# A hybrid decoder step on one core: weight splits on an absolute pace, waiting stores issued a step later, a third buffer for decay rows, sample states loaded ahead

## The chip, the cores and the metric

The kernel runs on one core of a Trainium2 chip. The metric is the time of one execution on the device in microseconds (us). The page below counts five engines: PE is TensorE's matmuls, PEld its weight loads, DVE is VectorE, ACT is ScalarE, POOL is GpSimd. SP is SyncE, which here does nothing but issue DMA transfers, one after the other; POOL issues some as well.

## The reference, cut to what matters

One layer: a half-step gated FFN, a token mixer of two gated branches (windowed pooling, and a state-space scan with a causal convolution), and a second half-step FFN, all in float32. There are 1024 prompt tokens and 8 sequences of 8 new tokens ("samples") that start from a stored state.

```
def swiglu(x, w_in, w_out):                     # D_MODEL 1024, D_FF 2816
    gu = x @ w_in
    g, u = gu[..., :D_FF], gu[..., D_FF:]
    return (jax.nn.silu(g) * u) @ w_out
def ssd_scan(x, dt, A, bm, cm, h0):             # 32 heads of 64, 4 groups, state 128, chunks of 128 tokens
    ...
    y_diag = jnp.einsum('bcgrls,bcsgrp->bclgrp', cb[:, :, :, None] * decay, xdt)
    st = jnp.einsum('bclgn,bclgr,bclgrp->bcgrpn', br, decay_end, xdt)
    h_last, h_prev = lax.scan(step, h0, ...)    # h * chunk_decay + st, chunk after chunk
    y_off = jnp.einsum('bclgn,bcgrpn,bclgr->bclgrp', cr, h_prev, jnp.exp(a_cs))
    return y_diag + y_off, h_last
def layer(x, pool_hist, out_pos0, conv_hist, h0, l):
    x = x + 0.5 * swiglu(rmsnorm(x, norm_ffn1[l]), ffn1_w_in[l], ffn1_w_out[l])
    mix, new_pool, new_conv, new_ssm = token_mixing(rmsnorm(x, norm_mix[l]), ...)
    x = x + mix
    x = x + 0.5 * swiglu(rmsnorm(x, norm_ffn2[l]), ffn2_w_in[l], ffn2_w_out[l])
    return x, new_pool, new_conv, new_ssm       # then a last rmsnorm
```

## The kernel before, in words

Tokens are cut into two halves, h = 0 (512 prompt tokens) and h = 1 (512 and the 64 sample tokens). Every weight and every operand is split into two parts, a rounded one (`wh`, `hi`, made by ACT) and the rest (`wl`, `lo`, made by DVE from the first), and a product is three matmuls: hi*wh, lo*wh, hi*wl. The wide projections use a seven-product scheme on 2x2 blocks (`wino`, tiles `pw`), whose block sums POOL makes (`s`, L443).

The stages, in order of time: **FFN 1 in** (products `pg`, `pu`, then `pw`; hidden rows go to DRAM as `hd`), **FFN 1 out** (`po`: first h = 0, then h = 1; hidden rows come back as `hr` through POOL's queue and are split into `hh` and `hr`), the **mixer's projections** (`pz`, `pw`: pool rows u, gate rows z, convolution rows, gates), the **mix stage** (the scan in 8 prompt chunks and one sample chunk for each of 4 groups, beside the pooling products `pgm` and `pbp`, the scan's output product `pso` and the merged output `pwo`), and **FFN 2**, built as FFN 1.

While FFN 1 runs, `part_weights` (L303) splits 90 weight pieces of the mixer and of FFN 2's start ahead of time: a load of 256 KB (`wr`), an ACT copy (`wp`, L352), a DVE subtraction (`wr`, L354), and two stores of 256 KB into DRAM (`wp<-wp`, `wp<-wr`, L314 and L315). Later stages load these pieces ready-made (`wraw<-wp`, `wh<-wp`, `wl<-wp`, L290).

The order on the engines comes from three things. The code is written as generators ("chains"). `pe[0]` is a clock that the program keeps while it is written out: each matmul adds its columns divided by 2400, so it runs in planned us, a little faster than the chip. A chain yields a delay, and `tick()`, called after each few matmuls, runs the chains that are due; a chain that is `finish`ed is written out at once, without matmuls between. Last, a scheduler places each engine's instructions by readiness and priority. Once placed, each engine, and SP's queue of transfers too, works strictly in its order: an instruction that waits holds everything behind it.

In the mix stage, `ssd_load` (L1277) loads the decay rows `ab` of a chunk, 512 KB, into one of two buffers. `ssd_a` (L1286) makes exponentials from them on ACT (`ea` L1299, eight Relu rows L1301, one Exp L1302), transposes x and B on PE (`pxT`, `pcb`) and copies B's transposition (`btok`, L1325). `ssd_m` multiplies `ab` by the masked products (L1337). `ssd_st` is the state product (`pst`); `ssd_b` makes the chunk's output (`pyo`, `pyd`). For the sample chunk `ssd_b` goes through eight units: load 256 KB of stored state (`h<-in_state_ssm_dram`, L1356), transpose (`ph0T`), products (`pyos`, `pnew`), add, store (`out_dram<-h`, L1389). `fin` (L1448, L1449) is the group's last prompt state. `gating` norms the result with `rstd` (a matmul `pss`, three Newton steps on DVE, a transposition `prt`, and a trip through DRAM, `rd` and `r`) and stores it as `yd`. In `u_pair`, POOL packs the last rows for the new pool state (`cst`, L984) and PE transposes them (`pust`).

Of the kernel before, what the change touches and what calls it, by code (L numbers as in the profile page):

```python
# [14 lines left out]
P = 128  # L15
# [46 lines left out]
G_WAIT = (4.0, 5.0)  # L62
H_AT, H_PACE, H_LAND = 2.0, (0.4, 0.68), 3.5
W_AT, W_LAND, W_NEXT = 105.0, 2.4, 1.7
# [3 lines left out]
def tile_hybrid_pool_ssd_macaron(  # L68
# [211 lines left out]
    def load_w(w, k0, nk, c0, ncol=P, raw=None, pin=False):  # L280
# [15 lines left out]
        with tc.high_priority(hp[0]):  # L296
            d = S.activation(wh, raw, AF.Copy)  # L297
            if pin:
                tc.keep_in_program_order(d)
            V.tensor_tensor(wl, raw, wh.bitcast(F32), op=ALU.subtract)  # L300
# [79 lines left out]
    def rstd(tiles, h, count, out, pace=1.0, sums=None, waits=None):  # L380
# [31 lines left out]
        S.copy(rt[:nch], pt[:nch, :P])  # L412
        dma(rd[:nch], rt[:nch])
# [189 lines left out]
    def ffn(wi, wo, prep, after, half=None, sums=None):  # L603
# [9 lines left out]
        def inner(h):  # L613


            N = NTOK[h]
            parts = [], []
            todo = []

            def cut():  # L620
                _, t, a = todo.pop(0)
                split(t, a[:, :N], t.bitcast(F32R))

            for k in range(NFF):
                own = k < 3 if h == 0 else not half and k >= NFF - 2
                t, a = (fx(d, n_) if own else act((P, 576), d, n_) for d, n_ in ((F32, "hr"), (F32R, "hh")))
                t = t[:, :N]
                G.dma_start(t, hdram[h][k])
                parts[0].append(a)
                parts[1].append(t.bitcast(F32R))  # L630
                todo.append((pe[0], t, a))
                yield H_PACE[h]
                while todo and todo[0][0] + H_LAND < pe[0]:
                    cut()
            while todo:
                yield max(0.3, todo[0][0] + H_LAND - pe[0])
                cut()
            return parts
# [7 lines left out]
        for h in HALVES:  # L646
# [3 lines left out]
            for ms in ((0, 1),) + tuple((m,) for m in range(2, KD)):  # L650
# [39 lines left out]
    def load_x(h, out):  # L690
# [31 lines left out]
        for i, (_, c0, c) in enumerate(blocks):  # L722
            V.tensor_scalar_mul(dg[i][:c, :c], ident[:c, :c], ss[:c, 2, i : i + 1])
        if h == 1:
# [86 lines left out]
    for _ in range(4):  # L811
# [152 lines left out]
    def u_pair(k0, sin, ost):  # L964
# [4 lines left out]
        def mean(h, k, raw):  # L969
# [5 lines left out]
            else:  # L975
# [8 lines left out]
                G.tensor_copy(st[:, HIST:].rearrange("p (b t) -> p b t", t=NT), raws[:, :, HIST:])  # L984
                pt = psum("ps", "pust")
# [199 lines left out]
    def load_dts(h):  # L1185

        t, cd = act((P, 480), name="dts"), small((P, 128), "cd", 2)
# [14 lines left out]
    def mix_pool(h):  # L1202
# [11 lines left out]

        def out(m):
            t0 = act((P, N), name="t0")
# [4 lines left out]
            dma(accd[h][m], t0)  # L1221
# [3 lines left out]
        for m in range(KD):  # L1225
# [8 lines left out]
            out(m)  # L1234

# [41 lines left out]

    def ssd_load(h, g, c):
# [453 lines left out]
```

## Time and profile before

| | us |
|---|---|
| median of 3 runs (lowest to highest) | 3009.23 (3006.12 to 3012.07) |
| the profiled execution | 3018.36 |
| its span, first to last instruction | 3016.4 |
| PE busy / DVE / ACT / POOL | 2877.0 / 1608.8 / 1314.1 / 858.0 |
| mean granted TensorE clock | 0.980 |

The page's second part shows the stages: each digit is the busy share of a fortieth of the span (75.4 us) in tenths.

```profile
PE   7999999898999999999999889998999999998998
...
PEclk9999999999999999999999989999999999999999
DMA  4487667896363333333368888788775222235442
```

Counted from 0, slices 7 to 9 are FFN 1 out and its two seams, slices 21 to 27 the mix stage, and slice 36 is the seam inside FFN 2. DMA is the busy share of the 16 engines that move the data.

### The profile page before, as it was taken

How to read it: one execution, taken by the hardware profiler on the slowest of the kernel's cores; microseconds unless marked ns; L12 is line 12 of the kernel's file. 1: busy time of each engine (PE TensorE's matmuls, PEld its weight loads, DVE VectorE, ACT ScalarE, POOL GpSimd, SP SyncE). 2: the span in 40 equal slices, each digit the busy share in tenths (PEclk: the TensorE clock that was granted, in tenths of full speed). 3: DMA queues.
4: the chain of work that ended last, by engine and by line, in shares of the span. 5: the costliest groups of instructions: out<-in, count | busy, mean ns of one | idle time of the engine just before them, and what ended most of it. 6: DMA issues, size and time to landing. Idle time of an engine off the chain costs nothing.

```text
span 3016.4 us, 54111 instructions
## 1 busy us (share of the span) xinstructions
PE 2877.0 (95%) x20356; PEld 2710.4 (90%) x20356; DVE 1608.8 (53%) x2834; ACT 1314.1 (44%) x2755; POOL 858.0 (28%) x917
## 2 busy tenths in 40 slices
PE   7999999898999999999999889998999999998998
PEld 6999999678989999999987787778999999997898
DVE  6554445545255576666647755663256343444532
ACT  5344444433233355555556745541123333343422
POOL 5333334000053333333313232342115333341000
PEclk9999999999999999999999989999999999999999
DMA  4487667896363333333368888788775222235442
GB/s 134 140 264 230 203 206 228 279 287 221 100 199 115 104 98 116 97 101 105 109 196 289 271 258 268 255 251 277 261 258 159 86 82 69 83 107 183 156 141 72
DMA packets 531225, 532.34 MB, mean 176 GB/s; under 512 B 41531, under 2 KB 371377, under 8 KB 530955
## 3 DMA queue, kind: packets, MB, share of 16 engines
q1 hardware_dynamic: 523906, 504.37, 52.5%
q0 software_dynamic: 7040, 24.52, 2.3%
q8 instruction: 160, 2.62, 0.4%
q14 instruction: 103, 0.84, 0.1%
q10 hardware_dynamic: 16, 0.00, 0.0%
HBM read 377.09 MB, written 151.90 MB: 175 GB/s over the span
## 4 chain that ended last, share of the span: by engine, by line
PE 75%; DMA 7%; issue 6%; DVE 4%; ACT 2%; POOL 2%; SPq 1%; ACTq 0%; DVEq 0%; POOLq 0%
PE pw L166 45%; PE po L166 10%; PE pso L166 6%; PE pwo L166 3%; PE pu L166 2%; PE pg L166 2%; DMA wr<-in_ffn_w_in_dram 1%; PE pbp L166 1%; PE pz L166 1%; DMA hr<-hd 1%; PE pyos L166 1%; DMA wraw<-wp 1%; PE pyd L166 1%; ACT ab L1301 1%; DMA wr<-in_w_o_dram 1%
## 5 line engine op out<-in xcount | busy, mean ns | idle before, releaser
L166 PE MATMUL pw<-hi,wh 128*128 128x288 f32 (+1 forms) x2176 | 630.6, 290 | 9.9 <-DVE t L554 9.5
L166 PE MATMUL pw<-hi,wl 128*128 128x288 f32 (+1 forms) x2176 | 628.9, 289 | 0.4 <-DVE wl L450 0.4
L166 PE MATMUL pw<-lo,wh 128*128 128x288 f32 (+1 forms) x2176 | 628.4, 289 | 0.0
L166 PE MATMUL pw<-X,wh 128*128 128x256 f32 (+1 forms) x3264 | 626.1, 290 | 2.1 <-ACT rb L842 1.3
L166 PEld LDWEIGHTS pw<-X,wh 128*128 128x128 f32 x3264 | 517.9, 191 | 3.2 <-ACT rb L842 1.7
L166 PE MATMUL pw<-X,wl 128*128 128x256 f32 (+1 forms) x1632 | 472.2, 289 | 0.1
L166 PEld LDWEIGHTS pw<-hi,wh 128*128 128x128 f32 x2176 | 412.8, 190 | 10.8 <-DVE t L554 10.2
L166 PEld LDWEIGHTS pw<-hi,wl 128*128 128x128 f32 x2176 | 412.8, 190 | 0.6 <-DVE wl L450 0.6
L166 PEld LDWEIGHTS pw<-lo,wh 128*128 128x128 f32 x2176 | 412.9, 190 | 0.0
L450 DVE TENSOR_TENSOR wl<-s,wh 128x512 fp32r<-128x512 f32 x284 | 204.9, 722 | 262.5 <-ACT wh L449 258.4
L166 PEld LDWEIGHTS pw<-X,wl 128*128 128x128 f32 x1632 | 311.8, 191 | 0.3 <-DVE wl L450 0.3
L443 POOL TENSOR_TENSOR s<-wraw,wraw 128x512 f32<-128x512 f32 x142 | 196.0, 1380 | 404.3 <-DVE wl L450 278.5
L166 PE MATMUL po<-hh,wh 128*128 128x288 f32 (+1 forms) x1056 | 292.4, 331 | 13.1 <-ACT wh L297 13.1
L449 ACT ACTIVATE wh<-s 128x512 fp32r<-128x512 f32 x284 | 179.7, 633 | 274.8 <-PE pw L166 220.5
L166 PE MATMUL po<-hh,wl 128*128 128x288 f32 (+1 forms) x1056 | 291.3, 331 | 5.2 <-DVE wl L300 4.6
L166 PE MATMUL po<-hr,wh 128*128 128x288 f32 (+1 forms) x1056 | 289.7, 329 | 0.0
L300 DVE TENSOR_TENSOR wl<-wraw,wh 128x512 fp32r<-128x512 f32 x216 | 142.5, 665 | 227.3 <-ACT wh L297 225.5
L297 ACT ACTIVATE wh<-wraw 128x512 fp32r<-128x512 f32 x216 | 127.1, 598 | 271.7 <-PE po L166 241.9
L450 DVE TENSOR_TENSOR wl<-wraw,wh 128x512 fp32r<-128x512 f32 x213 | 161.0, 756 | 104.0 <-ACT wh L449 96.3
L449 ACT ACTIVATE wh<-wraw 128x512 fp32r<-128x512 f32 x213 | 134.6, 632 | 179.9 <-PE pw L166 163.0
L166 PEld LDWEIGHTS po<-hh,wh 128*128 128x128 f32 x1056 | 181.0, 190 | 30.6 <-ACT wh L297 17.5
L166 PEld LDWEIGHTS po<-hh,wl 128*128 128x128 f32 x1056 | 180.4, 189 | 26.9 <-DVE wl L300 13.3
(390 smaller groups left out, 5204.9 us busy)
## 6 DMA issues: line engine op xcount, KB each, us to landing
wraw<-in_ffn_w_in_dram SPq DMA_DIRECT2D x184, 256.0 KB
wraw<-wp SPq DMA_DIRECT2D x180, 256.0 KB
wraw<-in_ffn_w_out_dram SPq DMA_DIRECT2D x160, 256.0 KB
wraw<-in_w_in_dram SPq DMA_DIRECT2D x124, 256.0 KB
wp<-wp SPq DMA_DIRECT2D x90, 256.0 KB
wp<-wr SPq DMA_DIRECT2D x90, 256.0 KB
wh<-wp SPq DMA_DIRECT2D x90, 256.0 KB
wl<-wp SPq DMA_DIRECT2D x90, 256.0 KB
```

The costliest lines, as they stand in the source:

```text
L166: T.matmul(out, lhsT, rhs, start=start, stop=stop, skip_group_check=free)
L297: d = S.activation(wh, raw, AF.Copy)
L300: V.tensor_tensor(wl, raw, wh.bitcast(F32), op=ALU.subtract)
L443: G.tensor_tensor(t, a, b, op=op)
L449: S.activation(wh, a, AF.Copy)
L450: V.tensor_tensor(wl, a, wh.bitcast(F32), op=ALU.subtract)
L1301: S.activation(ab[:L, i, :], ab[:L, i, :], AF.Relu, bias=acs[:L, hc + i : hc + i + 1], scale=-1.0)
```

## The change

It removes and adds no transfer: SP issues 1977 rows before and after, and the matmuls are the same. It moves work, in seven groups:

- **Start.** DVE subtracts the first three pinned weight pieces (`wl`) after the row norms of h = 0 instead of before them.
- **Early splits.** `part_weights` works on a pace of 4.3 planned us a piece from a fixed start; before, it waited 2.4 and then 1.7 after each step, and every wait rounded up to the next `tick`. Load, split and store of a piece are one step apart each, and a piece's store is written ahead of the next piece's split.
- **FFN out.** The hidden rows are split at a set pace, and the products of `po` start with the rows that are split, where before all 22 were split first.
- **Stores a step later.** `rd`, `accd`, `out_dram<-h`, `fin`, `yd` and `xspill` are written one step after the work that makes them.
- **Transpositions later.** `pust` four planned us after the packing; `pss` and `prt` of the gating by (5.0, 8.0) where it was (4.0, 5.0).
- **Decay rows.** A third `ab` buffer, and the load a chunk earlier. `cbm`, `btok` and `cd` move from a pool of their own into the 58 shared `act` slots. `btok` is copied ahead of the Relu rows.
- **Sample states.** The first three of a group are loaded when its sample chunk begins, and the two empty steps that stood between load and use are gone.

```diff
-G_WAIT = (4.0, 5.0)
-H_AT, H_PACE, H_LAND = 2.0, (0.4, 0.68), 3.5
-W_AT, W_LAND, W_NEXT = 105.0, 2.4, 1.7
+G_WAIT = (5.0, 8.0)
+H_AT, H_PACE, H_LAND, H_CUT = 2.0, (0.4, 0.68), 5.0, 0.9
+W_AT, W_NEXT = 108.0, 4.3
...
-        for w, k0, nk, c0, ncol in jobs:
-            t, a = fx(name="wr")[:, : nk * ncol], fx(F32R, name="wp")[:, : nk * ncol]
-            dma(t.rearrange("p (k c) -> p k c", c=ncol),
-                w[k0 * P : (k0 + nk) * P, c0 : c0 + ncol].rearrange("(k p) c -> p k c", p=P))
-            yield W_LAND
-            split(t, a, t.bitcast(F32R))
-            yield W_NEXT
-            d = dp.tile([P, 2, 4 * P], F32, tag=f"wp{len(parted)}", name=nm("wp"))
-            dma(d[:, 0, : nk * ncol], a.bitcast(F32))
-            dma(d[:, 1, : nk * ncol], t)
-            parted[id(w), k0, c0] = d
+        held, t0 = {}, pe[0]
+        for i in range(len(jobs) + 2):
+            if i < len(jobs):
+                w, k0, nk, c0, ncol = jobs[i]
+                t = fx(name="wr")[:, : nk * ncol]
+                dma(t.rearrange("p (k c) -> p k c", c=ncol),
+                    w[k0 * P : (k0 + nk) * P, c0 : c0 + ncol].rearrange("(k p) c -> p k c", p=P))
+                held[i] = t, fx(F32R, name="wp")[:, : nk * ncol]
+            if i >= 2:
+                ...
+                dma(d[:, 0, : nk * ncol], a.bitcast(F32))
+                dma(d[:, 1, : nk * ncol], t)
+                parted[id(w), k0, c0] = d
+            if 1 <= i <= len(jobs):
+                t, a = held[i - 1]
+                split(t, a, t.bitcast(F32R))
+            yield max(0.1, t0 + W_NEXT * (i + 1) - pe[0])
...
         S.copy(rt[:nch], pt[:nch, :P])
+        yield 1.0
         dma(rd[:nch], rt[:nch])
...
+            while k < NFF or todo:
+                if k < NFF:
+                    ...
+                    G.dma_start(t, hdram[h][k])
+                    todo.append((pe[0], t, a))
+                    k += 1
+                    yield H_PACE[h]
+                while todo and todo[0][0] + H_LAND < pe[0] and last + H_CUT < pe[0] or k == NFF and todo:
+                    if k == NFF:
+                        yield max(0.2, todo[0][0] + H_LAND - pe[0], last + H_CUT - pe[0])
+                    _, t, a = todo.pop(0)
+                    split(t, a[:, :N], t.bitcast(F32R))
+                    parts[0].append(a)
+                    parts[1].append(t.bitcast(F32R))
+                    last = pe[0]
...
-                    finish(hid[h])
-                    parts = hid[h].value
+                    hid[h].step() if not hid[h, "parts"] else None
+                    parts = hid[h, "parts"]
...
                         for kk in range(n4):
+                            while len(parts[0]) <= kb + kk:
+                                hid[h].step()
                             products([pts], wh, wl, kk, slice(0, P), [(h, *parts)], kb + kk, NFF)
...
+        if h == 0:
+            yield 0.0
...
-    for _ in range(4):
+    for _ in range(6):
         prep1[0][0].step()
...
                 G.tensor_copy(st[:, HIST:].rearrange("p (b t) -> p b t", t=NT), raws[:, :, HIST:])
+                yield 4.0
                 pt = psum("ps", "pust")
...
         def out(m):
+            if done:
+                later(1.5, lambda d=done.pop(): dma(*d))
             t0 = act((P, N), name="t0")
             ...
-            dma(accd[h][m], t0)
+            done.append((accd[h][m], t0))
...
-        ab = stage["p"].tile([P, HPG, P], F32, tag="ab", bufs=2, name=nm("ab"))[:, :, :L]
+        ab = stage["p"].tile([P, HPG, P], F32, tag="ab", bufs=3, name=nm("ab"))[:, :, :L]
...
-        cbm = small((P, P), "cbm", 2)
+        cbm = act((P, P), name="cbm")
...
-            h0s = {i: load(units[i]) for i in range(N_H0)}
-            yield STEP_S
-            yield STEP_S
             hTs = {0: turn(h0s[0], units[0])}
...
+                if last:
+                    dma(*last.pop())
                 dst = new_ssm_s[0, bh * 4 : bh * 4 + 4, 2 * gp : 2 * gp + 2].rearrange("b h p n -> (h p) b n")
-                dma(dst, h0)
+                last.append((dst, h0))
+            yield STEP_S
+            dma(*last.pop())
...
         for c in range(n):
-            a = yield from ssd_a(h, g, c, ab, Bf, Cf, xs4, dts)
+            cur = ab
+            if c + 1 < n:
+                ab = ssd_load(h, g, c + 1)
+            if c == 4:
+                for i in range(N_H0):
+                    h0s[i] = state_load(g, i)
+            a = yield from ssd_a(h, g, c, cur, Bf, Cf, xs4, dts)
             yield step
             if prev:
-                yield from ssd_b(h, g, *prev, Cf, y4, dts)
-            if c + 1 < n:
-                ab = ssd_load(h, g, c + 1)
+                yield from ssd_b(h, g, *prev, Cf, y4, dts, h0s)
...
             S.copy(fo, pt)
+            yield step
             dma(new_ssm_p[0, 0, g * HPG : (g + 1) * HPG].rearrange("(q h) p n -> (h p) q n", h=2),
...
-            dma(yd[h][k], y)
             yield GP[1]
+            if j:
+                dma(yd[h][k - 1], y4[:, j - 1, :N])
...
-            dma(xspill[h][m], x_)
+            if m:
+                dma(xspill[h][m - 1], out[m - 1])
```

Three places of the engines' order, before and now. In the rows a name left of the arrow is written, one right of it read; the numbers tell tiles apart.

ACT at the seam of FFN 1 in and FFN 1 out for h = 0, from the first hidden row (`hh<-hr`) on. `wp<-wr` is an early split, `wh<-wraw` a weight of `po`. Before:

```order
L352 ACTIVATE hh_6707<-hr_6706 128x512
L352 ACTIVATE wp_6734<-wr_6733 128x512
L352 ACTIVATE hh_6737<-hr_6736 128x512
L297 ACTIVATE wh_6931<-wraw_6929 128x512
L352 ACTIVATE hh_6758<-hr_6757 128x512
L352 ACTIVATE hh_6782<-hr_6781 128x512
L352 ACTIVATE hh_6809<-hr_6808 128x512
L557 ACTIVATE g_6683<-g_6683 128x288
L352 ACTIVATE hh_6839<-hr_6838 128x512
```

Now:

```order
L361 ACTIVATE hh_6830<-hr_6829 128x512
L361 ACTIVATE hh_6854<-hr_6853 128x512
L297 ACTIVATE wh_6968<-wraw_6966 128x512
L361 ACTIVATE wp_6879<-wr_6877 128x512
L361 ACTIVATE hh_6875<-hr_6874 128x512
L297 ACTIVATE wh_7038<-wraw_7036 128x512
L361 ACTIVATE hh_6905<-hr_6904 128x512
L567 ACTIVATE g_6800<-g_6800 128x288
L297 ACTIVATE wh_7068<-wraw_7066 128x512
```

The weights of `po` moved up among the hidden rows. Of the 90 early splits 62 stand ahead of the first row shown and 28 behind it before the change; now it is 78 and 12, the last of them behind 16 of h = 0's 48 weight pieces.

SP at the first sample chunk (group 0 of h = 1). Before, the three state loads stand behind eight loads of scan outputs (`y<-yd`):

```order
L1489 DMA y_21198<-yd_0_193 128x512
L1489 DMA y_21201<-yd_1_194 128x512
L1489 DMA y_21204<-yd_2_195 128x512
L1221 DMA accd_5_110<-t_3518_21101 128x576
L1489 DMA y_21207<-yd_3_196 128x512
L1489 DMA y_21210<-yd_4_197 128x512
L1489 DMA y_21213<-yd_5_198 128x512
L1489 DMA y_21216<-yd_6_199 128x512
L1489 DMA y_21219<-yd_7_200 128x512
L1356 DMA h_3551_21251<-in_state_ssm_dram 128x4x128
L1356 DMA h_3552_21253<-in_state_ssm_dram 128x4x128
L1356 DMA h_3553_21255<-in_state_ssm_dram 128x4x128
```

Now:

```order
L1549 DMA z_20983<-zd_148 128x576
L1302 DMA h_3497_20989<-in_state_ssm_dram 128x4x128
L1302 DMA h_3498_20991<-in_state_ssm_dram 128x4x128
L1302 DMA h_3499_20993<-in_state_ssm_dram 128x4x128
L290 DMA wl_21107<-wp_3541 128x512
L1499 DMA yd_12_205<-y_3310_20075 128x512
L1232 DMA accd_4_109<-t_3483_20935 128x576
```

They moved 24 rows up, ahead of all the loads of `y`.

SP after the last group's prompt state, in the output product of h = 0. Before, the store of `fin` stands ahead of the second half of the weight piece that PE is using (`wraw_23970`) and of all that follow:

```order
L1389 DMA out_dram<-h_4106_23814 128x4x128
L1389 DMA out_dram<-h_4110_23835 128x4x128
L1449 DMA out_dram<-fin_23956 128x4x128
L290 DMA wraw_23970<-wp_7390 128x512
L290 DMA wh_23991<-wp_7431 128x512
L290 DMA wl_23993<-wp_7431 128x512
```

Now:

```order
L1405 DMA out_dram<-h_4104_23802 128x4x128
L1409 DMA out_dram<-h_4110_23827 128x4x128
L1475 DMA out_dram<-fin_23954 128x4x128
L1619 DMA xspill_4_85<-x_4059_23587 128x512
L290 DMA wh_23988<-wp_6730 128x512
L290 DMA wl_23990<-wp_6730 128x512
```

The store still stands ahead of weight loads, but the first of them, `wh_23988`, is now the piece that PE reaches 15 matmuls after the transposition of `fin`; before, it was one that PE needed in the very next matmul.

On PE, `pust` stood one row behind the transposition `puh` of the same channel block (four of eight blocks) or 14 to 19 behind it; now it stands 25 to 37 rows behind.

More of the change, by code (lines that the diff above doesn't have):

```diff
@@ L616, in inner @@
             N = NTOK[h]
[L617 to L638, printed above, removed]
+            parts = hid[h, "parts"] = [], []
+            todo, last = [], 0.0
+            k = 0
+            while k < NFF or todo:
+                if k < NFF:
+                    own = k < 3 if h == 0 else not half and k >= NFF - 2
+                    t, a = (fx(d, n_) if own else act((P, 576), d, n_) for d, n_ in ((F32, "hr"), (F32R, "hh")))
+                    t = t[:, :N]
+                    G.dma_start(t, hdram[h][k])
[10 more added lines that the diff above has]
+                    last = pe[0]
         hid = {}
@@ L1185, in load_dts @@
     def load_dts(h):
-        t, cd = act((P, 480), name="dts"), small((P, 128), "cd", 2)
+        t, cd = act((P, 480), name="dts"), act((P, 128), name="cd")
         dma(t, dts_d[h][:, :480])
@@ L1234, in mix_pool @@
             out(m)
+        dma(*done.pop())
     def load_group(h, g):
@@ L1276, in sample_parts, with state_load @@
             yield STEP_S
+    SAMPLE_UNITS = [(pr, bh) for pr in range(4) for bh in range(2)]
+    def state_load(g, i):
+        pr, bh = SAMPLE_UNITS[i]
+        gp = g * 4 + pr
+        t = act((P, 4, P), name="h0")
+        dma(t, state_ssm[0, bh * 4 : bh * 4 + 4, 2 * gp : 2 * gp + 2].rearrange("b h p n -> (h p) b n"))
+        return t
     def ssd_load(h, g, c):
         L = NS if c == 4 else CH
-        ab = stage["p"].tile([P, HPG, P], F32, tag="ab", bufs=2, name=nm("ab"))[:, :, :L]
+        ab = stage["p"].tile([P, HPG, P], F32, tag="ab", bufs=3, name=nm("ab"))[:, :, :L]
         src = acs_sd[g * HPG : (g + 1) * HPG] if c == 4 else acs_d[h][c, g * HPG : (g + 1) * HPG]
@@ L1295, in ssd_a @@
         hcs = slice(hc, hc + HPG)
-        ea = act((P, 4, L), name="ea")
-        av = ab.rearrange("p (q h) l -> p q h l", h=2)
-        for hh in range(2):
-            S.activation(ea[hh * HD : (hh + 1) * HD], av[hh * HD : (hh + 1) * HD, :, hh, :], AF.Exp)
-        for i in range(HPG):
-            S.activation(ab[:L, i, :], ab[:L, i, :], AF.Relu, bias=acs[:L, hc + i : hc + i + 1], scale=-1.0)
-        S.activation(ab[:L], ab[:L], AF.Exp, scale=-1.0)
         px = psum("ps", "pxT")
@@ L1309, in ssd_a @@
             tr(pb[:L, 128:256], Bf[:, tok], ident)
+        ea = act((P, 4, L), name="ea")
+        av = ab.rearrange("p (q h) l -> p q h l", h=2)
+        for hh in range(2):
+            S.activation(ea[hh * HD : (hh + 1) * HD], av[hh * HD : (hh + 1) * HD, :, hh, :], AF.Exp)
+        btok = hn_ = None
+        if not smp:
+            btok = act((P, P), name="btok")
+            S.copy(btok, pb[:, 128:256])
+        for i in range(HPG):
+            S.activation(ab[:L, i, :], ab[:L, i, :], AF.Relu, bias=acs[:L, hc + i : hc + i + 1], scale=-1.0)
+        S.activation(ab[:L], ab[:L], AF.Exp, scale=-1.0)
         xd = act((P, 512), name="xd") if not smp else []
@@ L1323, in ssd_a @@
         else:
-            btok = small((P, P), "btok", 2)
-            S.copy(btok, pb[:, 128:256])
             hn_ = act((P, 512), name="hst")
@@ L1337, in ssd_m, with ssd_b @@
         V.tensor_tensor(ab[:L], ab[:L], cbm[:L, :L].unsqueeze(1).broadcast_to([L, HPG, L]), op=ALU.mult)
-    def ssd_b(h, g, c, a, hold, Cf, y4, dts):
+    def ssd_b(h, g, c, a, hold, Cf, y4, dts, h0s):
         dt, acs, dtd, cd, cdp = dts
@@ L1347, in ssd_b @@
             po = psum("ps", "pyos")
-            units = [(pr, bh) for pr in range(4) for bh in range(2)]
-            def src(u):
-                gp = g * 4 + u[0]
-                return state_ssm[0, u[1] * 4 : u[1] * 4 + 4, 2 * gp : 2 * gp + 2].rearrange("b h p n -> (h p) b n")
-            def load(u):
-                t = act((P, 4, P), name="h0")
-                dma(t, src(u))
-                return t
+            units, last = SAMPLE_UNITS, []
             def turn(h0, u):
@@ L1374, in ssd_b @@
                 if i + N_H0 < len(units):
-                    h0s[i + N_H0] = load(units[i + N_H0])
+                    h0s[i + N_H0] = state_load(g, i + N_H0)
                 yield STEP_S
@@ L1441, in ssd_group @@
         yield step
-        yield from ssd_b(h, g, *prev, Cf, y4, dts)
+        yield from ssd_b(h, g, *prev, Cf, y4, dts, h0s)
         if h == 1:
@@ L1588, in mix_out @@
                 V.tensor_tensor(x_[:, a:b], x_[:, a:b], pt[:, : b - a], op=ALU.add)
-            dma(xspill[h][m], x_)
+            if m:
+                dma(xspill[h][m - 1], out[m - 1])
             if h:
                 squares(sums, x_)
+        dma(xspill[h][KD - 1], out[KD - 1])
         return nxt, out
```

11 lines of the change are left out of this document (9 added, 2 removed).

## The prediction

> **What bounds the kernel now.** I read the page's busy shares first, then PE by stage, then PE's waits, and only then the queues behind each wait. PE is the engine to watch, and its busy row says little alone:
>
> ```profile
> PE 2877.0 (95%) x20356; PEld 2710.4 (90%) x20356; DVE 1608.8 (53%) x2834; ACT 1314.1 (44%) x2755; POOL 858.0 (28%) x917
> ```
>
> By stage (us from the span's start, then length, busy us of PE, PEld, DVE, ACT, POOL with counts, granted clock, DMA share, GB/s):
>
> ```profile
> 115.00:500.00 385.00, 384.62 (x3059) 383.96 (x3058) 192.22 (x356) 178.51 (x394) 133.79 (x108) 1.00 0.68 217
> 500.00:600.00 100.00, 87.19 (x456) 73.28 (x455) 58.57 (x93) 47.18 (x90) 21.12 (x32) 0.95 0.85 276
> 600.00:705.00 105.00, 88.73 (x404) 71.12 (x404) 48.97 (x89) 41.04 (x74) 9.73 (x19) 0.95 0.90 291
> 1100.00:1555.00 455.00, 454.58 (x3611) 452.43 (x3611) 303.64 (x543) 259.36 (x507) 165.87 (x228) 1.00 0.36 110
> 1555.00:1790.00 235.00, 212.21 (x1440) 176.89 (x1440) 162.67 (x287) 155.24 (x356) 63.13 (x50) 0.98 0.84 277
> 1790.00:1830.00 40.00, 35.55 (x165) 31.69 (x165) 12.35 (x20) 10.09 (x20) 12.71 (x12) 0.62 0.59 180
> 1830.00:2110.00 280.00, 260.73 (x1576) 215.97 (x1577) 164.82 (x272) 125.88 (x289) 92.58 (x75) 0.95 0.84 271
> 2300.00:2700.00 400.00, 400.00 (x3171) 400.00 (x3170) 158.48 (x282) 150.67 (x319) 130.47 (x115) 1.00 0.27 84
> 2700.00:2760.00 60.00, 51.60 (x281) 44.98 (x280) 35.35 (x56) 29.11 (x56) 21.46 (x35) 0.94 0.69 231
> 2760.00:2840.00 80.00, 80.00 (x361) 66.00 (x360) 31.07 (x49) 24.61 (x45) 0.00 (x0) 1.00 0.37 111
> 2840.00:2880.00 40.00, 38.14 (x246) 35.14 (x245) 25.02 (x51) 21.79 (x41) 7.47 (x14) 1.00 0.80 261
> ```
>
> The wide products (115 to 500, 1100 to 1555, 2300 to 2700) leave PE no gap: nothing is to be gained there, only lost. What can be gained lies at the seams of the FFNs and in the mix stage, where idle PE and a lowered clock go together. What PE itself waited for:
>
> ```profile
> PE ptx L166 <- DVE dg L723: 14.3, 1, 14.3
> PE po L166 <- ACT wh L297: 13.1, 8, 4.4
> PE pss L166 <- DVE ssq L378: 10.4, 1, 10.4
> PE pust L170 <- POOL cst L984: 8.5, 4, 3.7
> PE pwo L166 <- DMA wraw<-wp: 7.3, 1, 7.3
> PE prt L170 <- DVE rsm L367: 6.9, 4, 2.9
> PE ph0T L170 <- DMA h<-in_state_ssm_dram: 5.9, 2, 5.4
> PE po L166 <- DVE wl L300: 4.6, 5, 1.8
> PE pst L166 <- ACT btok L1325: 3.9, 5, 1.3
> PE pgm L166 <- DVE fl L356: 2.9, 1, 2.9
> PE pyd L166 <- DVE ab L1337: 2.6, 4, 0.8
> PE pbp L166 <- DVE fl L356: 2.5, 1, 2.5
> ```
>
> (total us, times, longest.) The change touches nearly every row of it.
>
> **The parts, each with its price.**
>
> *Start.* DVE's rows in order of time (start, us):
>
> ```profile
> 12.18 0.69 DVE L300 TENSOR_TENSOR wl<-wraw,wh 128x512 fp32r<-128x512 f32 x1
> ...
> 14.60 0.15 DVE L365 TENSOR_TENSOR xss<-xss 128x4 f32<-128x4 f32 x1
> ```
>
> Three subtractions stand in the middle of the chain that PE's 14.3 us wait for; behind the norms they run beside the `ptx` transpositions. 14.60 - 12.18 = 2.4 gained; between 0, if the first product then waits for `wl`, and 2.4. I take 2.4: the chain has nothing else in it.
>
> *`pust`.* It is moved 25 to 37 PE rows behind its partner. At 385/3059 = 0.126 us a matmul that is 3.1 to 4.7 us, against a longest wait of 3.7. The 8.5 go, and one of two clock dips of this stretch:
>
> ```profile
> 1050.00:1100.00 50.00, 45.28 (x330) 43.98 (x329) 31.14 (x60) 16.93 (x38) 14.88 (x19) 0.93 0.30 93
> ```
>
> 0.07 * 50 = 3.5 us of clock for both, 1.7 for one: 10.2 together (bounds 6 and 12).
>
> *Early splits.* 16 of the 90 move from FFN 1 out into FFN 1 in. What they do where they are:
>
> ```profile
> ACT wp L352 <- DMA wr<-in_ffn_w_in_dram: 35.4, 8, 11.0
> ...
> 660.67 3.50 DMA wr<-in_ffn_w_in_dram
> ...
> 678.01 13.71 DMA wr<-in_ffn_w_in_dram
> ```
>
> The first row is ACT from 600 to 705, the others are pieces of the chain that ended last. ACT stands still before a split whose load has not landed, and the weights of `po` queue behind it. At 678 the hidden rows of h = 1 flood the DMA, the load takes 13.71 us, ACT waits 11.0, and PE's 10.4 us before `pss` are the end of that. Now no split is left in 600:705. Its loss is 105 - 88.73 = 16.3 idle and 0.05 * 105 = 5.3 of clock, 21.6. FFN 2's out stage has the same code and no splits, and lost 0 in 2760:2840 and 1.9 in 2840:2880. I take 19. In 500:600 the loss is 12.8 + 5.0 = 17.8; FFN 2's seam (2700:2760) lost 8.4 + 3.6 = 12.0 without any split. Twelve splits still stand there, so I take half the difference, 3. The hidden rows on demand are in the same figure: the first `hr` subtraction on DVE still stands ahead of the last gate products, so the seam's own wait stays. Sum 22; bounds 0 and 19 + 17.8 = 37.
>
> What it costs in 115:500: 16 more pieces of 768 KB each way are 12.6 MB over 385 us, 33 GB/s on top of 217, share 0.68 to about 0.78, and 16 * 1.3 us of ACT and DVE, both half idle. Nothing, as long as weights still land early (rival 4).
>
> *Sample states.* The wait is 5.4. The clock of 1790:1830 lost 0.38 * 40 = 15.2. The three later groups do the same work in 1830:2110, which lost 0.05 * 280 = 14 for all three and more, 4.7 a group. So the wait brought about 10.5 of the 15.2: 15.9 together (bounds 5.4 and 20.6).
>
> The Trainium skill ("TensorE: Matmul & The Clock Gate", Part 1) says that the clock halves after an idle window of about 3.4 us and is back after one busy window of that length. By that rule the wait costs 5.4 + 1.7 and the whole sum is 62 instead of 71; this trace disagrees, with a mean clock of 0.62 over 40 us.
>
> *`fin`.* SP stood before the store, with a weight load behind it:
>
> ```profile
> 2065.89 0.37 SPq L1449
> ...
> 2066.36 6.16 DMA wraw<-wp
> ```
>
> The load starts 0.47 after the store and takes 6.16, which is the 7.3 of `pwo`. The store still stands ahead of loads, but PE has 15 matmuls more before the first of them, 15 * 80/361 = 3.3 us. I take 3.3 (bounds 0 and 7.3).
>
> *`prt`, `pss`.* The transposition follows its sum by 32 to 44 PE rows where it was 21 to 33: I take 5 of the 6.9 (0 to 6.9). Later `yd` stores: the products that read them come stages later, so nothing.
>
> *`btok`* is copied ahead of eight Relu rows: 3 of the 3.9. It pushes those rows back by one small copy (32 copies, 8.1 us of ACT busy in all); hidden, since `pyd` waits only 2.6 for `ab`, and at most 8.1 if not.
>
> *Third `ab`.*
>
> ```profile
> SPq L1283 <- PE pyd L166: 51.1, 19, 5.2
> SPq L1389 <- DVE h L1387: 49.4, 27, 5.8
> SPq L1471 <- DVE y L1470: 44.2, 27, 5.2
> ...
> ACT ea L1299 <- DMA ab<-acsd: 22.7, 10, 6.6
> ...
> by line: PE pbp L166 12.2%; ACT ab L1301 8.3%; DMA ab<-acsd 6.5%; POOL y L1456 5.5%; PE pyd L166 5.1%; PE pgm L166 4.9%; issue 4.6%; PE pst L166 3.6%; PE pw L166 3.5%; ACT ea L1299 3.4%; PE pyo L166 3.1%; DMA r<-rd 2.7%; DVE ab L1337 2.4%;
> ```
>
> SP waits 51.1 us before `ab` loads for a free buffer, 94 more before state and `yd` stores, all with weights behind. ACT then waits 22.7 for `ab`. On the chain of 1555:1790 these loads are 6.5% of 235, 15.3 us, the upper bound; the lower is 0. PE's own waits on what ACT is late with are 2.9 + 2.5 + 2.6 = 8.0 (`fl`, `fl`, `ab`), the nearest row: I take 7. Three tiles more in the shared `act` slots, and states that sit there longer, cost nothing while the `y` loads stand in SP's order where they did, which they do.
>
> *Seam of FFN 2:* weights ahead of the later hidden rows, 2 of the 2.8 us that the four `po` waits on DVE and ACT make there (0 to 4.4). *`rd` a step later:* up to one planned us for each norm, none on PE's path.
>
> Sum: 2.4 + 10.2 + 22 + 15.9 + 3.3 + 5 + 3 + 7 + 2 = 70.8. The profiled execution took 3018.4 (span 3016.4 and 2.0 around it), 9 above the median of 3009.2, so 2947.6 for it and **2938** for the median.
>
> **The rivals.**
>
> 1. *The mix stage keeps its waits.* The moved loads land later by what they start earlier, because the engines that move data are the limit there (0.84 busy at 277 GB/s). For it:
>
> ```profile
> 650.00:700.00 50.00, 38.29 (x178) 31.19 (x177) 25.39 (x49) 20.02 (x37) 9.73 (x19) 0.90 0.98 322
> ```
>
> At 0.98 a 256 KB load took 13.71 against 3.50. Against it: 277 is not 322, and SP's 145 us of waiting are its order, not bandwidth. The terms of this stage are 15.9 + 3.3 + 5 + 3 + 7 = 34.2; without them 2973. The Trainium skill ("Trainium Kernel Development and Optimization", Key Constraints) says that transfers from all queues run on the same 16 engines and interleave, so an earlier issue adds no bandwidth; the trace agrees at 0.98.
>
> 2. *The early splits give nothing back*: the twelve that remain hold ACT at the seam and PE is late from there on. For it, `po` waited for `wh` 13.1 us, the longest of them, 4.4, at the seam. 22 less: 2960.
>
> 3. *More than I count.* Idle PE in 1555:2110 is 22.8 + 4.5 + 19.3 = 46.6 and the clock 4.7 + 15.2 + 14 = 33.9, 80.5 in all; two thirds instead of 34.2 would be 20 more, and FFN 1's seam can give 15 more: 2903.
>
> 4. *Slower: the faster splits starve FFN 1 in.* Each of its 18 wide units needs four weight loads, issued when slots come free. If these land half as late as the one at 678 did, 5.1 us, and PE waits for it in every unit, that is 92: 3030. It decides from 70.8/18 = 3.9 us a unit. Against it, the same stretch in 40 slices:
>
> ```profile
> GB/s 127 164 160 180 315 293 199 284 181 321 280 294 180 247 317 199 189 208 260 151 226 150 209 233 263 133 225 255 185 213 145 266 186 252 153 233 223 214 175 187
> ```
>
> It has slices above 310 GB/s already, with PE 384.62 of 385 busy.
>
> **How the numbers follow.** My forecast, 2919 to 2958, 0.46; rival 1 (2959 to 3000) 0.22; rival 2 0.09; rival 3 0.13; rival 4 0.06; no change in sum, by gains and losses that I don't see, 0.04. About 0.2% (6 us) is what a measurement of this kernel can tell from no change. So faster 0.90, same 0.04, slower 0.06. The range reaches from rival 3's near part to most of rival 1: 2900 to 2985 (0.46 + 0.09 + 0.16 + 0.09 = 0.80).
>
> **What would show it.** After: no `wp` split behind the middle of h = 0's `po`, and 600:705's stretch like 2760:2880; no wait of `pust` above 0.5; `ph0T` not waiting for states, and the clock there above 0.8; SP's waits before `ab` loads near none; `pwo` still waiting some 4 us behind `fin`; PE full in FFN 1 in at a DMA share near 0.78. I am wrong if the mix stage moves at 0.9 share and PE waits for `wraw<-wp` instead, if FFN 1 in shows PE gaps, or if `po`'s seam waits grow.

## The result, and the profile after

The change made the kernel faster: 2962.13 us (median of 4 runs, 2958.05 to 2968.09) against 3009.57, a ratio of 0.9845 with a 95% interval of 0.9821 to 0.9868. On another chip the same kernel gave 2961.51 and 0.9829 (0.9805 to 0.9852). The forecast was 2938; the gain is 47.4 us where 71.2 were forecast.

The profiled execution has a span of 2956.3 us. It was the second fastest of its four (2958.12), and the one profiled before the change lies 8.8 above its median, so the two traces differ by 60.1 us, 12.7 more than the medians do. Both traces show 1975 transfers issued by SP: the number is the same before and after, though it is not the 1977 given above. PE's busy share rose to 97%:

```profile
PE 2855.2 (97%) x20356; PEld 2698.9 (91%) x20356; DVE 1634.7 (55%) x2834; ACT 1315.2 (44%) x2755; POOL 866.3 (29%) x917
```

Here is where the 60.1 us came from, cut at the same events of PE in both traces (the starts of the first `pw`, the first `po`, the first `pss` behind it, the first `pdt`, `pch` and `pgm` and the last `pwo`, then the end of the span):

| piece of the trace | before | changed | gain | forecast |
|---|---|---|---|---|
| start to first `pw` | 119.3 | 116.5 | 2.8 | 2.4 |
| FFN 1 in with its seam, to first `po` | 420.9 | 425.1 | -4.2 | 3 |
| FFN 1 out, h = 0, to `pss` | 154.9 | 125.9 | 29.0 | 19 |
| FFN 1 out, h = 1, to `pdt` | 138.4 | 136.2 | 2.2 | 0 |
| `pz` and u with `pust`, to `pch` | 261.4 | 253.1 | 8.3 | 10.2 |
| other projections, to `pgm` | 469.2 | 467.7 | 1.5 | 0 |
| mix stage, to the last `pwo` | 679.1 | 665.2 | 13.9 | 34.2 |
| FFN 2, to the end of the span | 773.2 | 766.6 | 6.6 | 2 |

Two rows carry the difference between forecast and result: the mix stage gave 20 us less than forecast, and the seam of FFN 1 lost where it was to gain. By stage, with the columns of before (from, to, length, busy us of PE, PEld, DVE, ACT, POOL, granted clock, DMA share, GB/s):

```profile
112.00:500.00 388.00, 387.21 (x3079) 386.55 (x3079) 220.19 (x376) 187.28 (x412) 135.19 (x109) 1.00 0.78 248
500.00:600.00 100.00, 87.62 (x468) 76.92 (x467) 59.27 (x94) 48.21 (x91) 25.37 (x39) 0.93 0.95 310
600.00:680.00 80.00, 79.92 (x410) 68.82 (x409) 41.22 (x73) 34.13 (x58) 5.96 (x12) 1.00 0.60 188
...
1515.00:1750.00 235.00, 214.24 (x1426) 177.24 (x1425) 171.27 (x287) 159.18 (x361) 74.58 (x53) 0.96 0.83 280
1750.00:1790.00 40.00, 37.51 (x241) 32.77 (x241) 18.51 (x30) 17.20 (x37) 13.55 (x12) 0.96 0.90 297
```

FFN 1 in stayed full with the faster splits (387.21 of 388, DMA share 0.78). The second row, with FFN 1's seam, lost as much as before (12.4 idle, clock 0.93); the third, FFN 1 out, lost nothing. The first stretch of the mix stage still has PE idle for 20.8 of 235 us, where before it was 22.8. In the stretch where PE reaches the first sample states the clock is 0.96 instead of 0.62. PE's longest waits show what took the old places:

```profile
PE pw L166 <- ACT t L562: 10.9, 1, 10.9
PE ptx L166 <- DVE dg L733: 10.8, 1, 10.8
PE pwo L166 <- DMA wh<-wp: 6.4, 1, 6.4
PE pw L166 <- DVE t L564: 6.1, 2, 4.6
PE pso L166 <- DMA wraw<-wp: 4.4, 2, 2.3
PE pyd L166 <- DVE ab L1365: 3.3, 3, 2.8
...
PE pust L170 <- POOL cst L996: 3.2, 3, 2.1
```

The waits of `po`, `pss` and `ph0T` are gone from the head of the list (`ph0T` still waits 0.6 us for states). At the head stands a wait that did not exist before, the last gate product of FFN 1 in waiting for ACT. ACT in order of time, just there:

```profile
522.56 0.38 ACT L560 COPY t<-pw 128x288 f32<-128x288 f32 x1
534.57 0.63 ACT L361 ACTIVATE wp<-wr 128x512 fp32r<-128x512 f32 x1 [11.64 <-DMA wr<-in_w_o_dram]
535.11 0.61 ACT L459 ACTIVATE wh<-wraw 128x512 fp32r<-128x512 f32 x1
535.63 0.38 ACT L562 COPY t<-pw 128x288 f32<-128x288 f32 x1
```

An early split stood still for 11.64 us, since its load landed late, and the copy `t` (L562) that the gate product needs stood behind it. It is a stall of the same kind as those that the change removed from FFN 1 out, now at its seam. SP's queue shows when the load was issued:

```profile
518.30 4.07 SPq L571 DMA_DIRECT2D hd<-g  x1
522.42 1.36 SPq L312 DMA_DIRECT2D wr<-in_w_o_dram  x1
```

It came behind a store of a hidden row whose issuing alone took 4.07 us, only just before ACT was free for the split, and then took 12 us to land, in a stretch with a DMA share of 0.95.

### The profile page after: what moved, and what is told of

Its sections match the earlier page's. It is cut to its first block, busy times and chain, and to the rows that moved or that the text cites. A ratio compares the mean times of both kernels' runs of the same rounds, so it can differ in the third digit from the quotient of the medians.

```text
span 2956.3 us, 54148 instructions
## 1 busy us (share of the span) xinstructions
PE 2855.2 (97%) x20356; PEld 2698.9 (91%) x20356; DVE 1634.7 (55%) x2834; ACT 1315.2 (44%) x2755; POOL 866.3 (29%) x917
## 5 line engine op out<-in xcount | busy, mean ns | idle before, releaser
L166 PE MATMUL pw<-hi,wh 128*128 128x288 f32 (+1 forms) x2176 | 631.3, 290 | 16.9 <-ACT t L562 10.9
L166 PEld LDWEIGHTS po<-hh,wl 128*128 128x128 f32 x1056 | 179.7, 189 | 14.3
```

Source lines behind the costliest of these rows:

```text
L166: T.matmul(out, lhsT, rhs, start=start, stop=stop, skip_group_check=free)
```

## The experiments

All ratios are to the kernel before, run on the same chip, with 95% intervals.

### The early splits, alone and undone

**Alone** on the kernel before:

```diff
-W_AT, W_LAND, W_NEXT = 105.0, 2.4, 1.7
+W_AT, W_NEXT = 108.0, 4.3
...  # part_weights as in the changed kernel, nothing else
```

> The kernel before with the new pace of the early splits and nothing else of the change. Theory A (the splits cost what ACT waits for their loads, wherever they stand): FFN 1 out for h = 0 loses its 25.8 us of stalls and low clock, one new wait of some 11 us for an early split appears at the seam before it, so 12 to 20 us faster than before, near 2993. Theory B (the hidden rows on demand bring the gain of FFN 1, the pace little): within 6 us of before, 3009.

Measured: 2989.74 against 3012.39, 0.993 (0.9912 to 0.9947), 22.7 us. The new wait is there with nothing else of the change present, and `po` waits only 2.4 us for `wh` on ACT, where it waited 13.1:

```profile
PE ptx L166 <- DVE dg L731: 13.3, 1, 13.3
PE pw L166 <- ACT t L560: 11.8, 1, 11.8
...
PE ph0T L170 <- DMA h<-in_state_ssm_dram: 4.8, 1, 4.8
```

**Undone** in the changed kernel (the same lines the other way):

> The changed kernel with the early splits as they were before. Theory A: FFN 1 out for h = 0 shows waits of ACT on wr loads and of po and pss again, 12 to 25 us slower than the changed kernel, 2974 to 2987. Theory B: within 6 us of the changed kernel, 2962.

Measured: 2984.64, 0.9906 (0.9887 to 0.9924), about 22 us slower than the changed kernel; its trace has 155.1 us in FFN 1 out for h = 0 again, instead of 125.9, and `po` waits for `wh` on ACT again:

```profile
PE po L166 <- ACT wh L297: 16.7, 5, 8.3
```

Theory A holds in both directions, a little above its range in the first: the splits' pace is worth 22 us, nearly half of what the change gained. The hidden rows on demand bring little in FFN 1 out: nothing without the pace (155.1 against 154.9 us for h = 0), and some 5 us with it (130.6 us with the pace alone, 125.9 in the changed kernel).

### The wait at the seam

```diff
-W_AT, W_NEXT = 108.0, 4.3
+W_AT, W_NEXT = 108.0, 3.6
```

> The changed kernel with the early splits at 3.6 planned us a piece instead of 4.3: all 90 stand ahead of the first hidden row. Theory A (the 10.9 us wait of the last gate product is an ACT split whose load lands late): that wait goes, 10 to 17 us faster than the changed kernel, 2945 to 2952, with DMA in FFN 1 in at 0.82 or more and PE still full. Theory C (the load is late since the hidden rows and weights fill the DMA there, and the gate product would wait anyway, or the faster splits starve FFN 1 in): 2960 or more.

Measured: 2951.37, 0.9795 (0.9778 to 0.9812), some 10 us faster than the changed kernel, at the slow end of theory A's range. The stretch to the first `po` is 419.5 instead of 425.1. FFN 1 in still holds PE full at a DMA share of 0.86:

```profile
115.00:500.00 385.00, 383.61 (x3052) 382.95 (x3051) 230.63 (x388) 194.55 (x423) 134.61 (x108) 1.00 0.86 277
500.00:545.00 45.00, 38.09 (x243) 35.47 (x242) 29.69 (x46) 25.66 (x51) 25.07 (x38) 0.89 0.88 297
```

The wait on ACT's split is gone, but 6.2 us of another wait stand in its place, for `t` (L564) on DVE, which stands behind the first hidden row. From POOL's, ACT's, DVE's and PE's rows in order of time:

```profile
521.47 0.54 POOL L635 DMA_DIRECT2D hr<-hd  x1 [1.31 <-DMA hd<-g]
529.39 0.63 ACT L361 ACTIVATE hh<-hr 128x512 fp32r<-128x512 f32 x1 [6.77 <-DMA hr<-hd]
530.05 0.69 DVE L363 TENSOR_TENSOR hr<-hr,hh 128x512 fp32r<-128x512 f32 x1 [6.99 <-ACT hh L361]
530.66 0.45 DVE L564 TENSOR_TENSOR t<-pw,t 128x288 f32<-128x288 f32 x1
531.16 0.61 PE L166 MATMUL pw<-hi,wh 128*128 128x288 f32 x1 [6.23 <-DVE t L564]
```

POOL issued that row's load at 521.47, after a store of a hidden row (`hd<-g`) had landed; ACT could split it 7.9 us later. Why it was issued so late, the order on POOL's queue tells (the number behind `hd0` is the row's):

```
L635 DMA hr_1193_7000<-hd0_3_228 128x512
L635 DMA hr_1198_7025<-hd0_4_229 128x512
...
L635 DMA hr_1229_7101<-hd0_16_241 128x512
L635 DMA hr_1177_6933<-hd0_0_225 128x512
L635 DMA hr_1183_6957<-hd0_1_226 128x512
L635 DMA hr_1188_6978<-hd0_2_227 128x512
```

The rows 0, 1 and 2, with which `po` begins and which ACT and DVE split first, are loaded behind fourteen others. Of the rows of h = 0 these three alone use slots of the `fx` pool, which in this order come free last.

**Held back instead of sped up:**

```diff
+            if i == 74:
+                t0 += 160.0
             yield max(0.1, t0 + W_NEXT * (i + 1) - pe[0])
```

> The changed kernel with the last 15 early splits held back until FFN 1 out works on h = 1, where DMA is at 0.48. Theory A: the seam's 10.9 us wait goes as well, and the splits cost nothing where their loads land in time: 10 to 17 us faster than the changed kernel, 2945 to 2952. Theory D (an early split in FFN 1 out costs po its weights wherever it stands, some 1 us each): 2960 to 2975.

Measured: 2956.89, 0.9815 (0.9797 to 0.9832). The seam gained (418.8), but FFN 1 out for h = 1, where the held splits went, took 142.8 us instead of 136.2, with PE waiting 4.3 us for the norm's `rsm` and ACT 7.0 us for `wr` loads. So the held splits were not free there, though DMA had been busy for only 0.48 of that stretch; with them it was 0.72. That is read from one trace, the slowest of the five executions (2962.99), and the interval overlaps the changed kernel's, so neither theory holds whole. Of the places tried, FFN 1 in is the one where the splits cost nothing.

### The mix stage: which part gained?

**Sample states loaded where they were:**

```diff
+            for i in range(N_H0):
+                h0s[i] = state_load(g, i)
+            yield STEP_S
+            yield STEP_S
             hTs = {0: turn(h0s[0], units[0])}
...
-            if c == 4:
-                for i in range(N_H0):
-                    h0s[i] = state_load(g, i)
```

> The changed kernel with the first three sample states of a group loaded where they were, with the two empty steps between load and use. Theory A (the term of the prediction, wait and low clock): 10 to 16 us slower than the changed kernel, 2972 to 2978, with a wait of ph0T for states of 5 us and a clock below 0.8 for some 40 us. Theory B (the stage is held by the data movement, so the states' wait only moves to another load): within 4 us of 2962.

Measured: 2953.33, 0.979 (0.9775 to 0.9805). **Two `ab` buffers, loaded where they were:**

```diff
-tag="ab", bufs=3
+tag="ab", bufs=2
...
-            if c + 1 < n:
-                ab = ssd_load(h, g, c + 1)
...
             a = yield from ssd_a(...)
...
                 yield from ssd_b(...)
+            if c + 1 < n:
+                ab = ssd_load(h, g, c + 1)
```

> The changed kernel with two ab buffers and the load of a chunk's decay rows where it was before. Theory A (SP's waits before these loads hold the weights): 5 to 10 us slower than the changed kernel, 2967 to 2972. Theory B (SP waits for the next store instead and the stage gains nothing from the third buffer): within 3 us of 2962.

Measured: 2956.21, 0.9803 (0.9788 to 0.9818). Neither kernel is slower than the changed one. Whether one is faster needed a second measurement of the changed kernel:

> The changed kernel itself, beside the others of this call and the kernel before on one chip, since undoing the sample states' or the decay rows' part gave 0.979 and 0.980 of the kernel before and the changed kernel 0.9845. Theory A (neither part is worth anything): 0.979 to 0.982 here. Theory B (each of them costs time): 0.983 to 0.987.

Measured: 2961.51, 0.9829 (0.9805 to 0.9852). That lies between the two theories: the intervals touch, so it is not shown that the two parts cost anything, though the mix stages of the two kernels, 664 and 662 us in their traces, are shorter than in all five traces that have the changed code there (665 to 670). It is shown that undoing either of them alone does not cost the 15.9 or the 7 us of the forecast. Why the states' wait does not come back can be read. Before, from the chain that ended last:

```profile
1782.56 0.83 DVE t L1220 x2
1783.39 0.02 issue
1783.40 0.32 SPq L1221
1783.72 0.05 issue
1783.77 0.42 SPq L1489
...
1787.52 5.20 DMA h<-in_state_ssm_dram
1792.72 0.14 issue
1792.86 2.09 PE ph0T L170 x8
```

SP's queue in order of time at the same place, with the states loaded where they were but the stores a step later:

```profile
1740.24 3.98 SPq L1519 DMA_DIRECT2D y<-yd  x8
1744.50 0.36 SPq L1502 DMA_DIRECT2D yd<-y  x1
1745.70 0.32 SPq L1232 DMA_DIRECT2D accd<-t  x1
1746.30 0.32 SPq L290 DMA_DIRECT2D wraw<-wp  x1
1746.95 1.83 SPq L1302 DMA_DIRECT2D h<-in_state_ssm_dram  x3
```

Before, SP waited until 1783.39 for DVE's `t`, to store `accd`; only then came five of the eight `y` loads and the states, and PE waited. The trace of the splits alone has the same chain at its place. With `accd` written a step later SP waits less than 1 us there, the states are issued 10 us ahead of PE's first `ph0T` at 1757.0, and PE waits 1.8 us for states in all. So two parts of the change took away the same wait, and undoing one leaves the other. This is read from the traces; a kernel with both undone was not run.

**All stores of the mix stage at once again** (the `dma` of `accd`, `out_dram<-h`, `fin`, `yd`, `xspill` back to the line that makes the tile, as in the diff of the change):

> The changed kernel with every store of the mix stage (accd, out_dram<-h, fin, yd, xspill) written at once again, as before. Theory A (the later stores bring what the mix stage gained, since SP then holds fewer weights back): 7 to 14 us slower than the changed kernel, most of it between the first pooling product and the last pwo. Theory B (SP waits for the same time one step later): within 4 us of the changed kernel.

Measured: 2965.75, 0.9849 (0.9828 to 0.987), 4.2 us slower than the changed kernel on that chip, with intervals that overlap, and between the ranges of the two theories. In its trace the mix stage takes 675.3 us, against 665.2 and 668.6 in the two traces of the changed kernel and 675.1 and 679.1 in the two traces with the old mix stage. That points to the later stores as what gained there, without proving it. What the moved transpositions, `btok` and `fin` gained by themselves was not run.

### Order or bytes?

**The sample-state stores from POOL's queue:**

```diff
                 if last:
-                    dma(*last.pop())
+                    G.dma_start(*last.pop())
...
             yield STEP_S
-            dma(*last.pop())
+            G.dma_start(*last.pop())
```

> The changed kernel with the 28 sample-state stores that are one unit late issued from POOL's queue instead of SP's, and the last of each group too. The bytes stay the same; SP's 42.5 us of waits before these stores go. Theory A (SP's order is the limit of the mix stage): 8 to 20 us faster than the changed kernel, 2942 to 2954, the 6.4 us wait of pwo gone with it. Theory B (the bytes are the limit): within 4 us of 2962, and pwo or pso wait as long for weights as before.

Measured: 2949.07, 0.9775 (0.9757 to 0.9793), 13 us faster than the changed kernel by the medians, 16 by the ratios (0.9775 and 0.9829), as theory A has it; the wait of `pwo` for a load is gone. **28 of the 32 stores left out** (so 28 pieces of the new states are missing from its results):

```diff
-                if last:
-                    dma(*last.pop())
+                last.clear()
```

> The changed kernel without 28 of the 32 sample-state stores (7.3 MB of the mix stage's 136 MB are left out, and so are SP's waits before them). Theory B (bytes are the limit): 7.3 MB at 274 GB/s are 27 us of transfer; 15 to 27 us faster than the changed kernel and clearly faster than the same stores on POOL's queue, 2935 to 2947. Theory A (SP's order): as fast as the stores on POOL's queue within 4 us. Theory C (PE waits for DVE, ACT and POOL there and neither counts): within 5 us of 2962.

Measured: 2935.01, 0.9732 (0.9714 to 0.975). The mix stage, in the order changed kernel, stores on POOL, stores left out:

```profile
1524.00:2190.00 666.00, 627.15 (x4121) 541.41 (x4121) 391.43 (x664) 316.10 (x703) 191.39 (x149) 0.96 0.83 275
```
```profile
1528.00:2181.00 653.00, 622.85 (x4120) 541.90 (x4119) 394.14 (x663) 314.73 (x702) 215.81 (x181) 0.97 0.84 280
```
```profile
1526.00:2166.00 640.00, 614.51 (x4121) 535.03 (x4119) 391.44 (x664) 315.26 (x702) 191.93 (x149) 0.98 0.82 275
```

The same bytes in another queue shorten the stage by 13 us, so SP's order holds transfers back. Leaving 7.3 MB out shortens it by another 13, half of the 26 that they take at 280 GB/s. That fits a stage which feels the bytes as well, but it does not show it: without the stores POOL is also busy for 24 us less than with them, and a state's tile comes free without waiting for its store. A last kernel (below) takes bytes out in another way.

SP's waits tell why taking away one of them yields so little. SP's longest rows in the mix stage, in the changed kernel and then with the stores on POOL:

```profile
SPq L290 <- PE pso L166: 56.5, 29, 3.8
SPq L1405 <- DVE h L1403: 42.5, 24, 6.0
SPq L1310 <- PE pyd L166: 40.8, 13, 6.4
```
```profile
SPq L290 <- PE pso L166: 64.2, 36, 4.4
SPq L1310 <- PE pyd L166: 56.3, 17, 10.6
```

The 42.5 us before the sample-state stores are gone, but the wait for `ab` buffers, 40.8 in the changed kernel, is 56.3, and the one for weight buffers went from 56.5 to 64.2. All rows of SP's waits in the mix stage add up to 361 us before, 347 and 355 in the two traces of the changed kernel and 353 with the stores on POOL. This reads as if SP waited for the pace of the stage, with its waits moving to the next row in line.

### A better kernel

```diff
-W_AT, W_NEXT = 108.0, 4.3
+W_AT, W_NEXT = 108.0, 3.6
...
-                    own = k < 3 if h == 0 else not half and k >= NFF - 2
+                    own = k >= NFF - 3 if h == 0 else not half and k >= NFF - 2
...  # and the sample-state stores from POOL's queue, as above
```

> Three edits of the changed kernel together: the early splits at 3.6 planned us, the sample-state stores from POOL's queue, and the three hidden rows of h = 0 that use slots of the fx pool are the last three instead of the first three (the first three were loaded behind 14 others, since those slots come free late, though po begins with them). Theory A (the gains are in different places and add): 11 + 13 + 5 us, 2930 to 2937 or 0.973, with no wait of pw at FFN 1's seam above 2 us. Theory B (they are the same time or the third does nothing): 2940 to 2948.

Measured: 2926.66 (2925.17 to 2929.89), 0.9723 (0.9702 to 0.9744): 35 us faster than the changed kernel on the same chip, and faster than theory A's range: at least the three gains together (10, 13 to 16, and some 5 forecast for the third edit, which was not run alone). No wait of `pw` is left at the head of PE's list, and the seam keeps PE idle for 2.8 of 40 us at full clock:

```profile
PE ptx L166 <- DVE dg L733: 11.3, 1, 11.3
PE pyd L166 <- DVE ab L1365: 4.5, 3, 3.6
PE prt L170 <- DVE rsm L376: 4.3, 5, 2.3
```
```profile
500.00:540.00 40.00, 37.18 (x253) 34.82 (x252) 33.10 (x50) 27.10 (x54) 22.48 (x33) 1.00 0.88 283
```

The stretch to the first `po` is 414.2 us instead of 425.1 (419.5 with the faster splits alone), and FFN 2's wide products, from the first `pw` to the first `po`, take 404.1 instead of 408.9 in the changed kernel's trace from this chip: the same `inner` loads FFN 2's hidden rows.

**With fewer bytes in the mix stage:**

```diff
-    early += [(wz, kb, 4, m * P, P) for m in range(KD) for kb in (0, 4)]
...  # with the edits of the better kernel, but W_NEXT = 4.3
```

> The kernel with the stores from POOL and the last three rows in fx, but at the pace of 4.3, and without the 16 early splits of w_o (pwo): each of these pieces is loaded as 256 KB and split on the spot instead of 512 KB ready-made, twice. 8.4 MB less in and behind the mix stage, 12.6 MB less in FFN 1, 32 splits of 0.6 us of ACT and 0.7 of DVE more in the mix. Theory A (the mix stage is held by bytes): as fast as the one with all 90 or up to 10 us faster. Theory B (ACT and DVE are needed there): 5 to 20 us slower than that one.

Measured: 2932.98, 0.9738 (0.9715 to 0.976), 6 us slower by the medians, with intervals that overlap. The mix stage of the better kernel, then of this one:

```profile
1511.00:2163.00 652.00, 622.14 (x4119) 542.94 (x4118) 394.44 (x663) 315.00 (x702) 215.31 (x181) 0.96 0.83 280
```
```profile
1508.00:2169.00 661.00, 625.99 (x4120) 545.71 (x4121) 417.24 (x695) 332.07 (x734) 217.45 (x181) 0.96 0.80 264
```

It moves 661 * 0.264 = 174.5 MB where the better kernel's moves 652 * 0.280 = 182.6, and takes 8 to 9 us longer, with 23 us more of DVE and 17 of ACT. (The five traces with one and the same mix code spread over 5 us.) A stage held by bytes alone would have gone the other way. That DVE and ACT, though idle for a third and half of it, stand on the way of PE there too is the likely reading; the extra splits also make SP wait, 22.7 us before raw weights for DVE's `wl`, and the two were not told apart.

## Why the prediction was right, and where it was wrong

**Direction and range** held (2900 to 2985), and 2962 lies in the band given to rival 1, the mix stage keeping its waits (2959 to 3000, 0.22), not in the forecast's own (2919 to 2958). Rival 2 names 2960, but its reason is excluded: the early splits alone brought 22 us. The step that failed is the mix stage's part of the sum: 34.2 forecast, 13.9 in the two traces, and 10 if all the traces of each form are taken (mean 677 of 2 with the old mix code, 667 of 5 with the new one and no change in it). That the time still fell into the range is in part luck, since FFN 1 out and FFN 2 gained 15 us more than their terms, against 7 less at the seam.

- *Start*: 2.4 forecast, 2.8 measured; the wait of `ptx` fell from 14.3 to 10.8.
- *`pust`*: 10.2 forecast, 8.3 in the traces. 3.2 us of its waits stayed, longest 2.1, where none above 0.5 was expected.
- *Early splits*: 22 forecast; 22.7 alone, about 22 when undone. The sum is right by two errors. FFN 1 out for h = 0 gained 29.0, not 19: some 24 by the pace alone, the rest only with the hidden rows on demand. The seam lost 4.2 where I had put a gain of 3. I counted the twelve splits behind the first hidden row and took half of the difference to FFN 2's seam; but two more stand ahead of that row, in front of the last gate copies on ACT, where one late load stops PE for 10.9 us. The first `hr` subtraction was named as the seam's own wait; it is what stands in line next (6.2 us), and its cause is the slot that its load waits for.
- *Sample states*: 15.9 forecast, nothing when undone alone. Two steps failed. The wait of 5.4 is real, and 4.8 in the trace of the splits alone; but I gave the whole of it to the states' move ahead of the `y` loads, when the `accd` store among those loads was what SP waited at, and another part of the change moved that. And the 10.5 us of clock were read from one trace: it has the clock at half for 30.7 us there, but the trace of the splits alone, with the same code at that place, for 13.7. A clock dip of one execution is no price.
- The Trainium skill ("TensorE: Matmul & The Clock Gate", Part 1) has the clock halve after an idle window of some 3.4 us and return after one busy window. Its length fits many dips: in the mix stages of all 14 traces the granted clock goes to half 119 times, 55 times for 3.4 us, 50 times for 6.8, and 14 times for longer, up to the 30.7 us above, through most of which PE was busy. Its condition fits fewer: of the eight dips before the change five came behind idle stretches of PE of only 1.6 to 2.9 us. The sum by that rule, 62, was nearer to the result than mine, but not for its reason, since undoing the term that it prices otherwise cost nothing.
- *`fin`*: 3.3 forecast, 0.9 in the traces: `pwo` waits 6.4 instead of 7.3. The 15 matmuls covered 3.4 us, as I had counted, but the chain behind `fin` grew: SP issued the weight load 4.1 us after the transposition instead of 1.1, behind four stores, of which an `xspill` store alone took 1.27 us to issue. I saw that a store still stood ahead of the weights, and took its price as unchanged.
- *`prt`, `pss`*: 5 forecast; `prt` waits 2.1 instead of 6.9, and `pss` no longer waits 2.6 for the squares. *`btok`*: 3 forecast; its 3.9 us of waits fell to 0.2. Most of these waits went, and the stage did not shorten by as much; none of the three was undone alone.
- *Third `ab`*: 7 forecast, nothing when undone. SP's wait before those loads fell from 51.1 to 40.8 only, and in the kernel with two buffers it is 56.9, with ACT waiting 50.2 us for `ab` instead of 16.6, and the time does not change. The three rows of PE's waits that I took as the nearest price, 8.0 us before, are 8.4 in the changed kernel: the third buffer did not end them.
- *Seam of FFN 2*: 2 forecast, with 4.4 as the bound; FFN 2 gained 6.6, 1.1 of it from the first `pw` to the first `po` and 5.5 behind. The term was too small, and no run tells which edit brought it.
- *Rival 4*, starving FFN 1 in, did not come: PE is full at 0.78 and, at 3.6 a piece, at 0.86. *Rival 2* was near in its reason (a split does hold ACT at the seam, though not one of the twelve behind the first hidden row) and wrong in its price.
- The **profiled execution** was 9 us slower than its median. I took the same 71 off the median, though the extra 9 us can lie in the very stalls that are counted. The trace of the splits alone has 4 us less in a mix stage of the same code.

What stays open: which edits brought the 10 to 14 us of the mix stage (the later stores are the likely ones) and the 6.6 of FFN 2; how the rest of the mix stage's sensitivity divides between bytes and the engines' own chains; and whether the states' and the decay rows' parts cost a few us or nothing. The `pust` and start terms are read from the two traces, and were not run alone.

## What to carry to other kernels

A wait in an in-order queue belongs to the first instruction that stands still, not to the loads between it and the late one. Before you price a removed wait, follow the queue back to where it stopped, and ask which other edit already moves that; the two do not add. Where a queue waits in hundreds of small pieces, taking one kind of wait away can move most of it to the next kind; here the stage shortened clearly where work was taken out of the queue, or out of the program. When work is moved away from a stall, look for the last piece that stays at the edge: one late load stalled the seam by 10.9 us until all pieces were clear of it. Read the price of a clock dip from more than one trace.

## What the runs showed of the hardware

- The DMA engines carried 277 GB/s at a share of 0.86 beside a PE busy for 383.61 of 385 us, so FFN 1 in had room for all 90 splits.
- The same stores moved from SP's queue to POOL's cost POOL 24 us more of busy time (191 to 216) and shortened the mix stage by 13 us (666 to 653).
- The granted clock's dips at one place, in kernels with the same code there, differ between traces: 30.7 us at half clock in one, 13.7 in another.
- Five of the eight dips in the mix stage before the change followed idle stretches of PE of 1.6 to 2.9 us.
